# Attention steps of 512 score columns: nine steps a head pair in place of twelve, with the scan's state kept as a column

## The chip, the core and the metric

The kernel runs on one core of a Trainium2 chip. The metric is device time in microseconds (us) of one execution. The core has a matrix engine (TensorE, PE in the profile, with its weight loads as PEld), three engines for elementwise work (VectorE or DVE, ScalarE or ACT, GpSimd or POOL) and a queue that issues the transfers (SyncE or SP). PE writes to PSUM alone; POOL works on SBUF alone.

## The reference, cut to what matters

A trunk of two layers over 1024 positions of width 1024: a Mamba-2 layer, a shared projection to K and V, and one layer of stick-breaking attention with 16 heads of 64, then a norm. The change touches the attention alone. For each block of 128 queries:

```python
z = jnp.einsum('bthd,bshd->bhts', q[:, lo:hi], k[:, :hi]) * scale
mask = (query position > key position)
log_keep = jnp.where(mask, jax.nn.log_sigmoid(-z), 0.0)
after = lax.cumsum(log_keep, axis=3, reverse=True) - log_keep
log_a = jnp.where(mask, jax.nn.log_sigmoid(z) + after, -jnp.inf)
a = jnp.exp(log_a)
outs.append(jnp.einsum('bhts,bshd->bthd', a, v[:, :hi]))
```

The weight of a key is thus sigmoid(z) times the product of sigmoid(-z) over all later keys that the query may see. The kernel computes that product as a running product (a scan) from the last key to the first.

## The kernel before, in words

Everything ahead of the attention (about the first 1010 us) and behind it is the same in both kernels.

**Work of the attention.** Heads go in eight pairs p. A pair has eight query blocks i of 128 queries, and the keys are cut into two halves c of 512. A *piece* (i, c) is block i against half c: block 6 has the pieces (6,1), 384 columns wide, and (6,0), 512 wide; block 2 has (2,0) alone, 384 wide. The piece that holds the diagonal is a *top* piece; for a block with two pieces the upper half (c = 1) is done first, since the running product goes from the last key down. A pair has twelve pieces with 36 x 128 columns.

**A step** is one piece in `scores` (L819) and, LAG = 3 steps later, in `transposes` (L849).
- `scores`: PE multiplies for both heads into the PSUM tile `sc` (L828; one buffer of two banks). ACT reads it twice, sigmoid(-z) into `kp` (L830) and sigmoid(z) into `be` (L831). For a top piece POOL masks the diagonal 128 columns of both (L835) and sets the end column of `kp` to 1 (L837). For the other pieces it copies the first column of the upper piece's `kp` into that place (L839). DVE scans `kp` in place, once for each head (L841); the scan of a lower piece starts from the first column of the upper one's `kp`, which `above` remembers as a whole tile. POOL multiplies `be` with `kp` shifted by one column (L846).
- `transposes`: PE transposes the 128-column blocks of `be` into a PSUM tile `at` for each head (L856; two buffers). ACT empties the first head's (L860), DVE the second's (L858), into the SBUF tile `aT` of the block pair t = i // 2.
- `av` (L862): one step after the last piece of a block pair has been transposed, PE multiplies `aT` with V (L869), and DVE multiplies the result with the gate (L872).

**Filler.** Between these, PE runs the projections to queries and gates (`qproj` L768, `zproj1` L780), and at the end part of the output projection (`oproj` L794), as a generator: each `next` is one *yield* of three matmuls with 512 columns. For each weight, ACT makes the rounded copy and POOL the residual (`lq`, `lqz`, L124 and L125, four pieces each).

**Order.** PE's order is the program's (a manual schedule); the other engines' instructions are ordered by the compiler's scheduler. The main loop (L905) does for step n, with `rate` = `rates[n % 12]`:

```python
transposes(...)                      # of step n - 3
for _ in range((rate + 1) // 2): next(fl, None)
for r in now: av(*r[1])
live[n] = scores(p, i, c)
for _ in range(rate // 2): next(fl, None)
```

The `order` of pieces and `rates` (L900 to L902) are written out by hand and sum up to 32 yields a pair.

Of the kernel before, what the change touches and what calls it, by code (L numbers as in the profile page):

```python
# [12 lines left out]
F32 = mybir.dt.float32  # L13
F32R = mybir.dt.float32r
AF = mybir.ActivationFunctionType
ALU = mybir.AluOpType
# [3 lines left out]
P = 128  # L20
# [4 lines left out]
HT = T // NH  # L25
# [7 lines left out]
AVD = 1  # L33
# [19 lines left out]
def tile_trunk(ctx, tc, xT, c, vec, ada0, adar, wxbc, wwave, wdt, wz, wmo, wk, wv, wq, wqz, wso, out):  # L53
    nc = tc.nc
    V, S, Q, E, Y = nc.vector, nc.scalar, nc.gpsimd, nc.tensor, nc.sync
# [58 lines left out]
    def mm_tile(name):  # L114
        return pmm.tile([P, HT], F32, tag="mm", name=name)
# [43 lines left out]
    with ExitStack() as es:  # L159
# [9 lines left out]
                        channel_multiplier=-1)  # L169
# [97 lines left out]
        def wave_mm(d, hf):  # L267
            for m in range(NW):
# [12 lines left out]
                               op1=ALU.mult)  # L281
# [148 lines left out]
        order = []  # L430
# [23 lines left out]
    with ExitStack() as es:  # L454
# [30 lines left out]
        st = [pst.tile([P, 512], F32, name=f"st{g}") for g in range(G)]  # L485
# [128 lines left out]
        for n, (i, cc) in enumerate(todo):  # L614
            u = units[i]
            c = u["hf"] * CPH + cc
# [28 lines left out]
    with ExitStack() as es:  # L645
# [27 lines left out]
        for hf in range(NH):  # L673
# [3 lines left out]
            for d in range(ND):  # L677
# [19 lines left out]
            ps = pp.tile([P, HT], F32, tag="ss", name=f"ss1_{hf}")  # L697
# [15 lines left out]
        for hf in range(NH):  # L713
            hs = slice(hf * HT, (hf + 1) * HT)
            for m in range(8):
                wh, wl = load_w(wk[m], f"k{m}_{hf}")
                ps = mm_tile(f"pk{m}_{hf}")
# [7 lines left out]
            for ch in range(2):  # L725
                ps = [pp.tile([P, 512], F32, tag=f"v{s}", name=f"pv{s}_{ch}_{hf}") for s in range(4)]
# [35 lines left out]
    with ExitStack() as es:  # L762
        pa = pool(es, "p5", bufs=2)
        pp = pool(es, "pp5", bufs=2, space=PSUM)
        pone = pp.tile([P, 1], F32, name="pone", bufs=1)
# [50 lines left out]
        hsl = [slice(64 * a, 64 * a + 64) for a in range(2)]  # L816


        def scores(p, i, c):  # L819
            kd, q = pairs[p][0], qs[p]  # L820
            n = f"{p}_{i}_{c}"
            w = min(P * (i + 1), HT * (c + 1)) - HT * c
            top = HT * c + w == P * (i + 1)
# [3 lines left out]
            for a in range(2):  # L827
                E.matmul(ps[:, a, 0:w], q[hsl[a], i * P:(i + 1) * P], kd[hsl[a], HT * c:HT * c + w],  # L828
                         start=True, stop=True)
            S.activation(kp[:, :, 0:w], ps[:, :, 0:w], AF.Sigmoid, scale=-0.125)  # L830
            S.activation(be[:, :, 0:w], ps[:, :, 0:w], AF.Sigmoid, scale=0.125)  # L831
            if top:
                dg = slice(w - P, w)
                for t, fill in ((kp, 1.0), (be, 0.0)):
                    Q.affine_select(out=t[:, :, dg], in_=t[:, :, dg], pattern=[[0, 2], [-1, P]],  # L835
                                    compare_op=ALU.is_gt, fill=fill, base=0, channel_multiplier=1)
                Q.memset(kp[:, :, w:w + 1], 1.0)  # L837
            else:
                Q.tensor_copy(kp[:, :, w:w + 1], above[p, i][:, :, 0:1])  # L839
            for a in range(2):  # L840
                V.tensor_tensor_scan(out=kp[:, a, 0:w][:, ::-1], data0=kp[:, a, 0:w][:, ::-1],  # L841
                                     data1=pone.to_broadcast([P, w]),
                                     initial=1.0 if top else above[p, i][:, a, 0:1], op0=ALU.mult,
                                     op1=ALU.mult)
            above[p, i] = kp
            Q.tensor_tensor(out=be[:, :, 0:w], in0=be[:, :, 0:w], in1=kp[:, :, 1:w + 1], op=ALU.mult)  # L846
            return be

        def transposes(p, i, c, be, at):  # L849
            n = f"{p}_{i}_{c}"  # L850
            m = min(i + 1 - 4 * c, 4)
            tc_ = slice((i % 2) * P, (i % 2 + 1) * P)
            for a in range(2):
                ps = pp.tile([P, 4, P], F32, tag="at", name=f"at{n}_{a}", bufs=2)
                for j in range(m):
                    E.transpose(ps[:, j, :], be[:, a, j * P:(j + 1) * P], ident)  # L856
                if a:
                    V.tensor_copy(at[:, a, 0:m, tc_], ps[:, 0:m, :])  # L858
                else:
                    S.copy(at[:, a, 0:m, tc_], ps[:, 0:m, :])  # L860

        def av(p, t, at):  # L862
            vd, g = pairs[p][1], gs[p]
# [18 lines left out]
        qs, szs, pairs, gs, above = {}, {}, {}, {}, {}  # L882
# [20 lines left out]
        steps = [(p, *ic) for p in range(8) for ic in order]  # L903
        live, rows, ready = {}, {}, []
        for n in range(len(steps) + LAG + AVD):  # L905
            rate = rates[n % 12]
            m = n - LAG
            now, ready = [r for r in ready if r[0] <= n], [r for r in ready if r[0] > n]
            if 0 <= m < len(steps):
                p, i, c = steps[m]  # L910
                t = i // 2
                if (p, t) not in rows:
                    rows[p, t] = [pa.tile([P, 2, 4, 256], F32, tag="aT", name=f"aT{p}_{t}_{b}", bufs=3)
                                  for b in range((2 * t + 5) // 4)]
                transposes(p, i, c, live.pop(m), rows[p, t][c])
                if i % 2 == 1 and c == 0:
                    ready.append((n + AVD, (p, t, rows.pop((p, t)))))
            for _ in range((rate + 1) // 2):
                next(fl, None)
            for r in now:  # L920
                av(*r[1])
            if n < len(steps):
                p, i, c = steps[n]
                if n % 12 == 0:
# [3 lines left out]
                live[n] = scores(p, i, c)  # L928
            for _ in range(rate // 2):
                next(fl, None)  # L930
        for _ in fl:
# [3 lines left out]
    with ExitStack() as es:  # L935
# [25 lines left out]
        for hf, c0, c1, ds in ((1, 0, 512, (0, 5, 1, 2, 3, 4, 6, 7)), (0, 0, 256, (6, 7, 0, 1, 2, 3, 4, 5)),  # L961
                               (0, 256, 512, (6, 7, 0, 1, 2, 3, 4, 5))):
            w = c1 - c0
            last = hf == 0 and c0 > 0
            n = f"{hf}_{c0}"
# [6 lines left out]
            for i, d in enumerate(ds):  # L972
                if hf == 0:
                    t = x2t[:, i, :]
                elif d < NPRE:
                    t = x2p[d]
                else:
                    t = pf.tile(sh, F32, tag=f"x2_{d}", name=f"x2_{d}", bufs=1)
                if hf == 0 or d >= NPRE:
                    Y.dma_start(out=t, in_=x1_d[d][hf][:, c0:c1])  # L980
                if hf == 1 and d == NPRE:
                    ps = part[d][0]
                elif hf == 1 and d < NPRE:
                    ps = mm_tile(f"ps{d}_{n}")
                else:
                    ps = pp.tile([P, HT], F32, tag="pq", name=f"ps{d}_{n}", bufs=4)[:, 0:w]
# [4 lines left out]
                else:  # L991
# [3 lines left out]
                    for k in range(ND):  # L995
# [3 lines left out]
                                       op1=ALU.add)  # L999
# [93 lines left out]
```

## Time and profile before

| | us |
|---|---|
| median of three runs | 1516.09 (1509.9 to 1516.46) |
| the profiled execution's own time | 1520.12 |
| its span in the profile | 1518.4 |
| attention stage, first scores to last product | about 1012 to 1440 of the span |
| PE busy in the whole span | 1450.6 |

Engines are named as above. In the views, a group of instructions has the line of the kernel, the engine, the operation and its tiles (out<-in), and a row's bracket tells how long the engine had been idle before it and what ended that. Matmuls are pipelined, and the ends that the profile gives them are modelled, so a row's duration for a matmul is longer than the distance to the next matmul's start. An f32 matmul is recorded as two.

### The profile page before, as it was taken

The page shows a single profiled execution, that of the slowest core. Times are in us where ns is not written, and L with a number is a line of the kernel's source. Part 1 is how long each engine was busy: PE and PEld are TensorE (multiplying, and loading weights), DVE is VectorE, ACT ScalarE, POOL GpSimd, SP SyncE. Part 2 cuts the span into 40 slices and gives each one's busy share as a digit, 9 for nine tenths or more (in the row PEclk, how much of TensorE's full clock was granted, in tenths as well). Part 3 has the DMA queues.
Part 4 walks back from the last instruction along what each step waited for, and adds up shares of the span by engine and source line. Part 5 has one row for each costly group of instructions (what it writes and reads, how often), then busy time and mean ns, then how long its engine had stood idle before and what let it go on. Part 6 is the DMA issues. An engine that isn't in the chain of part 4 may idle for free.

```text
span 1518.4 us, 20697 instructions
## 1 busy us (share of the span) xinstructions
PE 1450.6 (96%) x7538; PEld 1113.8 (73%) x7538; DVE 989.7 (65%) x1221; ACT 746.4 (49%) x1273; POOL 563.1 (37%) x613
## 2 busy tenths in 40 slices
PE   4799999999998899999999999999999999999997
PEld 2587887888776788788888888876666666666787
DVE  5989974545789888976733427225665666667564
ACT  5554446235767666733523325244454545455542
POOL 2821220002655566522011000046565656556532
PEclk8899999999999999999999999999999999999999
DMA  9278884234566766658433446441121212112252
GB/s 337 86 247 292 286 297 153 98 110 127 180 219 211 215 213 211 197 170 285 151 121 124 139 139 193 130 141 43 49 77 43 62 44 70 36 37 89 82 186 101
DMA packets 104581, 227.36 MB, mean 150 GB/s; under 512 B 9488, under 2 KB 40992, under 8 KB 103456
## 3 DMA queue, kind: packets, MB, share of 16 engines
q1 hardware_dynamic: 104480, 226.04, 45.4%
q8 instruction: 60, 0.98, 0.3%
q14 instruction: 41, 0.34, 0.1%
HBM read 184.32 MB, written 41.68 MB: 149 GB/s over the span
## 4 chain that ended last, share of the span: by engine, by line
PE 60%; DVE 10%; issue 4%; POOL 4%; ACT 3%; DMA 2%; DVEq 0%; POOLq 0%; ACTq 0%; SPq 0%
DVE kp L841 4%; PE av L869 4%; PE po L132 4%; PE po L130 4%; PE po L131 4%; PE sc L828 3%; PE at L856 3%; PE pr L132 2%; PE pz L130 2%; PE pr L131 2%; PE pr L130 2%; PE pk L130 2%; PE pv L137 2%; PE pk L132 2%; PE pv L135 2%
## 5 line engine op out<-in xcount | busy, mean ns | idle before, releaser
L846 POOL TENSOR_TENSOR be<-be,kp 128x768 f32<-128x768 f32 (+3 forms) x96 | 148.6, 1548 | 149.2 <-DVE kp L841 128.4
L830 ACT ACTIVATE kp<-sc 128x768 f32<-128x768 f32 (+3 forms) x96 | 78.3, 815 | 183.7 <-PE sc L828 157.2
L841 DVE TENSOR_TENSOR_SCAN kp<-kp,pone 128x512 f32<-128x512 f32 (+3 forms) x128 | 97.9, 807 | 80.6 <-POOL kp L835 79.6
L130 PE MATMUL pr<-h0h,hx 128*128 128x512 f32 x336 | 131.8, 392 | 5.0 <-ACT hx L124 2.5
L132 PE MATMUL pr<-h0h,lx 128*128 128x512 f32 x336 | 131.7, 392 | 0.5 <-DVE lx L125 0.5
L131 PE MATMUL pr<-h0l,hx 128*128 128x512 f32 x336 | 131.5, 391 | 0.0
L505 ACT ACTIVATE lm<-lm,nac 128x128 f32<-128x128 f32 x256 | 78.6, 389 | 57.9 <-POOL lm L502 57.9
L130 PE MATMUL pz<-h0h,hz 128*128 128x512 f32 x256 | 105.9, 414 | 0.0
L841 DVE TENSOR_TENSOR_SCAN kp<-kp,kp,pone 128x512 f32<-128x512 f32 x64 | 78.5, 1268 | 40.4 <-ACT kp L830 40.4
L132 PE MATMUL po<-yh,lo 128*128 128x512 f32 x256 | 101.0, 395 | 1.3 <-DVE lo L125 1.3
L131 PE MATMUL po<-yl,ho 128*128 128x512 f32 x256 | 101.5, 397 | 0.5 <-DVE yl L665 0.5
L130 PE MATMUL po<-yh,ho 128*128 128x512 f32 x256 | 100.7, 393 | 1.3 <-ACT ho L124 1.3
L132 PE MATMUL pz<-h0h,lz 128*128 128x512 f32 x256 | 100.5, 392 | 1.0 <-DVE lz L125 1.0
L131 PE MATMUL pz<-h0l,hz 128*128 128x512 f32 x256 | 100.1, 391 | 0.0
L125 POOL TENSOR_TENSOR lq<-rq,hq 128x256 fp32r<-128x256 f32 x32 | 22.7, 739 | 178.4 <-ACT hq L124 178.4
L856 PE MATMUL at<-ident,be 128*128 128x128 f32 x576 | 82.5, 277 | 6.3 <-POOL be L846 5.0
L828 PE MATMUL sc<-kd,q 64*128 64x512 f32 (+3 forms) x384 | 88.0, 535 | 0.0
L533 POOL TENSOR_TENSOR xwl<-xw,xwh 128x512 fp32r<-128x512 f32 x20 | 26.8, 1341 | 163.2 <-ACT xwh L531 153.6
L856 PEld LDWEIGHTS at<-ident,be 128*128 128x128 f32 x576 | 66.1, 141 | 25.3 <-POOL be L846 8.0
L340 DVE SCALAR_TENSOR_TENSOR cv<-pr,vt,cv 128x1023 f32<-128x1023 f32 (+2 forms) x63 | 80.4, 1277 | 0.9
L124 ACT CAST ho<-ro 128x1024 fp32r<-128x1024 f32 x32 | 33.7, 1053 | 89.9 <-PE po L131 81.3
L130 PEld LDWEIGHTS pr<-h0h,hx 128*128 128x128 f32 x336 | 63.5, 189 | 19.1 <-ACT hx L124 2.9
(258 smaller groups left out, 3921.6 us busy)
## 6 DMA issues: line engine op xcount, KB each, us to landing
ar<-adar SPq DMA_DIRECT2D x48, 512.0 KB, 5.3
lm<-ac_d SPq DMA_DIRECT2D x32, 512.0 KB, 4.9
rz<-wz SPq DMA_DIRECT2D x32, 512.0 KB, 3.9
ro<-wmo SPq DMA_DIRECT2D x32, 512.0 KB, 3.5
xs_d<-sv SPq DMA_DIRECT2D x24, 512.0 KB, 3.4
rx<-wxbc SPq DMA_DIRECT2D x21, 512.0 KB, 4.9
x<-xT SPq DMA_DIRECT2D x32, 256.0 KB, 5.4
a<-ada SPq DMA_DIRECT2D x8, 1024.0 KB, 7.4
```

What stands on the lines that cost most here:

```text
L124: S.copy(h[:, i:i + n, :], r[:, i:i + n, :])
L130: E.matmul(ps, wh, xh, start=first, stop=False)
L131: E.matmul(ps, wh, xl, start=False, stop=False)
L132: E.matmul(ps, wl, xh, start=False, stop=last)
L340: V.scalar_tensor_tensor(out=ac[:, i:], in0=ps[:, :T - i], scalar=vv("cw", m * 4 + 3 - i), in1=ac[:, i:], op0=ALU.mult, op1=ALU.add)
L505: S.activation(lm[:, h, :], lm[:, h, :], AF.Exp, bias=nac[:, c, h0_ + h:h0_ + h + 1])
L828: E.matmul(ps[:, a, 0:w], q[hsl[a], i * P:(i + 1) * P], kd[hsl[a], HT * c:HT * c + w], start=True, stop=True)
L830: S.activation(kp[:, :, 0:w], ps[:, :, 0:w], AF.Sigmoid, scale=-0.125)
L841: V.tensor_tensor_scan(out=kp[:, a, 0:w][:, ::-1], data0=kp[:, a, 0:w][:, ::-1], data1=pone.to_broadcast([P, w]), initial=1.0 if top else ...
L846: Q.tensor_tensor(out=be[:, :, 0:w], in0=be[:, :, 0:w], in1=kp[:, :, 1:w + 1], op=ALU.mult)
L856: E.transpose(ps[:, j, :], be[:, a, j * P:(j + 1) * P], ident)
L869: E.matmul(ps[hsl[a], cs], vd[:, j, hsl[a]], at[j // 4][:, a, j % 4, cs], start=j == 0, stop=j == nj - 1)
```

## The change

Pieces are put together so that each step has exactly 512 columns: (6,1) with (0,0), (1,0) with (5,1), (4,1) with (2,0), and six pieces that are 512 wide alone. A generator `pieces` gives for each piece of a step its width w, its offset o in `sc` and `be`, its offset ok in `kp` (one column more for each piece, for its end column) and whether it is a top piece. In `scores`, PE, the first sigmoid, masks, scans and products go piece by piece; the second sigmoid covers the whole step. For an upper piece POOL copies the first column of its scan into a small tile of its own, which takes the place of the whole `kp` in `above`. In `transposes` four blocks are transposed for each head, and the evictions go piece by piece. The tiles `aT` have four buffers in place of three and are allocated one by one. The order and the rates are new. The diff, cut to its core:

```diff
+        def pieces(step):
+            o = 0
+            for b, (i, c) in enumerate(step):
+                w = min(P * (i + 1), HT * (c + 1)) - HT * c
+                yield i, c, w, o, o + b, HT * c + w == P * (i + 1)
+                o += w
+
-        def scores(p, i, c):
+        def scores(p, step):
...
-            kp = pa.tile([P, 2, HT + 1], F32, tag="kp", name="kp" + n, bufs=3)
+            kp = pa.tile([P, 2, HT + 2], F32, tag="kp", name="kp" + n, bufs=3)
...
-            S.activation(kp[:, :, 0:w], ps[:, :, 0:w], AF.Sigmoid, scale=-0.125)
-            S.activation(be[:, :, 0:w], ps[:, :, 0:w], AF.Sigmoid, scale=0.125)
...
+            for i, c, w, o, _, _ in pieces(step):
+                for a in range(2):
+                    E.matmul(ps[:, a, o:o + w], q[hsl[a], i * P:(i + 1) * P],
+                             kd[hsl[a], HT * c:HT * c + w], start=True, stop=True)
+            for _, _, w, o, ok, _ in pieces(step):
+                S.activation(kp[:, :, ok:ok + w], ps[:, :, o:o + w], AF.Sigmoid, scale=-0.125)
+            S.activation(be, ps, AF.Sigmoid, scale=0.125)
+            for i, c, w, o, ok, top in pieces(step):
+                end = kp[:, :, ok + w:ok + w + 1]
+                if top:
...
+                else:
+                    Q.tensor_copy(end, above[p, i])
+                for a in range(2):
+                    ka = kp[:, a, ok:ok + w][:, ::-1]
+                    V.tensor_tensor_scan(out=ka, data0=ka, data1=pone.to_broadcast([P, w]),
+                                         initial=1.0 if top else above[p, i][:, a, 0:1], op0=ALU.mult,
+                                         op1=ALU.mult)
+                if c == 1:
+                    above[p, i] = pa.tile([P, 2, 1], F32, tag="ab", name=f"ab{p}_{i}", bufs=5)
+                    Q.tensor_copy(above[p, i], kp[:, :, ok:ok + 1])
+                Q.tensor_tensor(out=be[:, :, o:o + w], in0=be[:, :, o:o + w],
+                                in1=kp[:, :, ok + 1:ok + w + 1], op=ALU.mult)
...
-                for j in range(m):
+                for j in range(4):
                     E.transpose(ps[:, j, :], be[:, a, j * P:(j + 1) * P], ident)
...
+                for i, c, w, o, _, _ in pieces(step):
...
+                    at = rows[p, t][c][:, a, 0:m, (i % 2) * P:(i % 2 + 1) * P]
+                    if a:
+                        V.tensor_copy(at, ps[:, o:o + m, :])
+                    else:
+                        S.copy(at, ps[:, o:o + m, :])
...
-        order = [(6, 1), (6, 0), (7, 1), (7, 0), (0, 0), (1, 0), (4, 1), (4, 0), (5, 1), (5, 0), (2, 0),
-                 (3, 0)]
-        rates = (3, 4, 4, 4, 1, 1, 1, 4, 2, 3, 2, 3)
...
+        order = [((6, 1), (0, 0)), ((6, 0),), ((7, 1),), ((7, 0),), ((1, 0), (5, 1)), ((4, 1), (2, 0)),
+                 ((4, 0),), ((5, 0),), ((3, 0),)]
+        rates = (4, 4, 4, 4, 2, 4, 4, 3, 3)
```

## Rows read from the trace of the kernel before

**Rows 1.** The page, first part: busy us of each engine, share, instructions

```profile
PE 1450.6 (96%) x7538; PEld 1113.8 (73%) x7538; DVE 989.7 (65%) x1221; ACT 746.4 (49%) x1273; POOL 563.1 (37%) x613
```

**Rows 2.** Windows: two periods of one head pair, and four us in the seventh

```profile
core 0: us, PE busy (x) PEld busy (x) DVE busy (x) ACT busy (x) POOL busy (x), PEclk, DMA share, GB/s
...
1109.45:1161.51 52.06, 51.37 (x298) 33.32 (x296) 31.79 (x45) 26.46 (x46) 30.78 (x49) 1.00 0.18 57
1161.51:1213.58 52.07, 51.38 (x298) 33.33 (x297) 31.80 (x45) 26.46 (x46) 30.79 (x49) 1.00 0.19 55
...
1372.00:1376.00 4.00, 3.34 (x14) 2.35 (x16) 4.00 (x4) 2.90 (x5) 3.08 (x3) 0.73 0.06 23
```

**Rows 3.** Timeline of PE around the step after piece (0,0): start us, us, what

```profile
1130.29 0.47 PE L130 MATMUL pq<-h1h,hq 128*128 128x512 f32 x1
...
1131.16 0.49 PE L828 MATMUL sc<-kd,q 64*128 64x128 f32 x4
1131.58 0.66 PE L856 MATMUL at<-ident,be 128*128 128x128 f32 x4
1132.40 0.66 PE L856 MATMUL at<-ident,be 128*128 128x128 f32 x4 [0.16 <-DVE aT L858]
1132.81 0.48 PE L130 MATMUL pq<-h1h,hq 128*128 128x512 f32 x1
```

**Rows 4.** Timeline of PE up to the transposes of piece (2,0) and behind

```profile
1157.53 0.50 PE L130 MATMUL pqz<-h1h,hqz 128*128 128x512 f32 x1
...
1158.33 1.04 PE L856 MATMUL at<-ident,be 128*128 128x128 f32 x8
1159.12 0.48 PE L130 MATMUL pqz<-h1h,hqz 128*128 128x512 f32 x1
...
1160.67 0.92 PE L828 MATMUL sc<-kd,q 64*128 64x384 f32 x4
1161.51 0.50 PE L130 MATMUL pqz<-h1h,hqz 128*128 128x512 f32 x1
...
1163.00 0.88 PE L856 MATMUL at<-ident,be 128*128 128x128 f32 x6 [0.53 <-POOL be L846]
...
1167.73 0.70 PE L828 MATMUL sc<-kd,q 64*128 64x512 f32 x2
```

**Rows 5.** Timeline of PE at the same place of the seventh pair

```profile
1369.78 0.50 PE L130 MATMUL pqz<-h1h,hqz 128*128 128x512 f32 x1
...
1372.66 0.88 PE L856 MATMUL at<-ident,be 128*128 128x128 f32 x6 [1.92 <-POOL be L846]
...
1378.96 1.13 PE L828 MATMUL sc<-kd,q 64*128 64x512 f32 x4
```

**Rows 6.** Timelines of DVE and POOL before piece (2,0)'s transposes; line 754: ns min/median/max

```profile
1159.45 1.80 DVE L841 TENSOR_TENSOR_SCAN kp<-kp,pone 128x384 f32<-128x384 f32 x2 [3.84 <-POOL kp L835]
...
1156.20 2.12 POOL L125 TENSOR_TENSOR lq<-rq,hq 128x256 fp32r<-128x256 f32 x3
...
L754 DVE TENSOR_TENSOR gl<-gr,gh x14: 667/684/2491, 1364.4 to 1453.7; 128x512 fp32r<-128x512 f32 x14
```

**Rows 7.** Groups by form in the period 1109.45 to 1161.51: busy us, mean ns

```profile
L831 ACT ACTIVATE be<-sc 128x1024 f32<-128x1024 f32 x6 | 6.1, 1019 | 0.0
...
L835 POOL TENSOR_SCALAR_AFFINE_SELECT kp<-kp 128x256 f32<-128x256 f32 x8 | 3.3, 413 | 0.3 <-ACT kp L830 0.3
...
L841 DVE TENSOR_TENSOR_SCAN kp<-kp,pone 128x256 f32<-128x256 f32 x4 | 2.5, 675 | 1.5 <-POOL kp L835 1.4
...
L846 POOL TENSOR_TENSOR be<-be,kp 128x512 f32<-128x512 f32 x2 | 2.2, 1090 | 2.2 <-DVE kp L841 2.2
...
L830 ACT ACTIVATE kp<-sc 128x512 f32<-128x512 f32 x2 | 1.2, 600 | 2.9 <-PE sc L828 2.9
...
L839 POOL COPY kp<-kp 128x2 f32<-128x2 f32 x4 | 0.8, 188 | 0.0
```

**Rows 8.** The chain of waits: the product with V of blocks 6 and 7

```profile
1138.28 3.39 PE av L869 x32
```

More of the change, by code (lines that the diff above doesn't have):

```diff
@@ L825, in scores @@
             be = pa.tile([P, 2, HT], F32, tag="be", name="be" + n, bufs=4)
             ps = pp.tile([P, 2, HT], F32, tag="sc", name="sc" + n, bufs=1)
-            for a in range(2):
-                E.matmul(ps[:, a, 0:w], q[hsl[a], i * P:(i + 1) * P], kd[hsl[a], HT * c:HT * c + w],
-                         start=True, stop=True)
-            S.activation(kp[:, :, 0:w], ps[:, :, 0:w], AF.Sigmoid, scale=-0.125)
-            S.activation(be[:, :, 0:w], ps[:, :, 0:w], AF.Sigmoid, scale=0.125)
[L832 to L846, printed above, removed]
-            return be
@@ new lines, in scores @@
+            S.activation(be, ps, AF.Sigmoid, scale=0.125)
+            for i, c, w, o, ok, top in pieces(step):
+                end = kp[:, :, ok + w:ok + w + 1]
+                if top:
+                    for t, e, fill in ((kp, ok + w, 1.0), (be, o + w, 0.0)):
+                        t = t[:, :, e - P:e]
+                        Q.affine_select(out=t, in_=t, pattern=[[0, 2], [-1, P]],
+                                        compare_op=ALU.is_gt, fill=fill, base=0, channel_multiplier=1)
+                    Q.memset(end, 1.0)
+                else:
[10 more added lines that the diff above has]
+                                in1=kp[:, :, ok + 1:ok + w + 1], op=ALU.mult)
@@ L853, in transposes @@
+            return be
+        def transposes(p, step, be):
+            n = f"{p}_{step[0][0]}_{step[0][1]}"
             for a in range(2):
                 ps = pp.tile([P, 4, P], F32, tag="at", name=f"at{n}_{a}", bufs=2)
-                for j in range(m):
+                for j in range(4):
                     E.transpose(ps[:, j, :], be[:, a, j * P:(j + 1) * P], ident)
[L857 to L860, printed above, removed]
+                for i, c, w, o, _, _ in pieces(step):
+                    t, m, o = i // 2, w // P, o // P
+                    if (p, t) not in rows:
+                        rows[p, t] = {}
+                    if c not in rows[p, t]:
+                        rows[p, t][c] = pa.tile([P, 2, 4, 256], F32, tag="aT", name=f"aT{p}_{t}_{c}",
+                                                bufs=4)
+                    at = rows[p, t][c][:, a, 0:m, (i % 2) * P:(i % 2 + 1) * P]
[3 more added lines that the diff above has]
+                        S.copy(at, ps[:, o:o + m, :])
@@ L899, in tile_trunk @@
             next(fl)
-        order = [(6, 1), (6, 0), (7, 1), (7, 0), (0, 0), (1, 0), (4, 1), (4, 0), (5, 1), (5, 0), (2, 0),
-                 (3, 0)]
-        rates = (3, 4, 4, 4, 1, 1, 1, 4, 2, 3, 2, 3)
-        steps = [(p, *ic) for p in range(8) for ic in order]
+        order = [((6, 1), (0, 0)), ((6, 0),), ((7, 1),), ((7, 0),), ((1, 0), (5, 1)), ((4, 1), (2, 0)),
+                 ((4, 0),), ((5, 0),), ((3, 0),)]
+        rates = (4, 4, 4, 4, 2, 4, 4, 3, 3)
+        ns = len(order)
+        steps = [(p, st) for p in range(8) for st in order]
         live, rows, ready = {}, {}, []
         for n in range(len(steps) + LAG + AVD):
-            rate = rates[n % 12]
+            rate = rates[n % ns]
             m = n - LAG
@@ L909, in tile_trunk @@
             if 0 <= m < len(steps):
[L910 to L917, printed above, removed]
+                p, st = steps[m]
+                transposes(p, st, live.pop(m))
+                for i, c in st:
+                    if i % 2 == 1 and c == 0:
+                        ready.append((n + AVD, (p, i // 2, rows.pop((p, i // 2)))))
             for _ in range((rate + 1) // 2):
@@ L922, in tile_trunk @@
             if n < len(steps):
-                p, i, c = steps[n]
-                if n % 12 == 0:
+                p, st = steps[n]
+                if n % ns == 0:
                     gs[p] = pa.tile([P, T], F32, tag="g", name=f"g{p}", bufs=1)
@@ L927, in tile_trunk @@
                         pairs[p + 1] = load_pair(p + 1)
-                live[n] = scores(p, i, c)
+                live[n] = scores(p, st)
             for _ in range(rate // 2):
```

8 lines of the change are left out of this document (1 added, 7 removed).

## The prediction

> **What bounds the kernel now.** I read the page first, then the attention stage pair by pair, then TensorE's own queue. The page has PE (TensorE) busy for 96% of the span [rows 1]. A busy PE is not proof of a full one, so the second view cuts the attention stage into head pairs. From the second pair on the pattern repeats every 52.06 us (six periods, all 52.04 to 52.09; two stand here): PE is busy for 51.4 us of it, DVE (VectorE) for 31.8, POOL (GpSimd) for 30.8, ACT (ScalarE) for 26.5 [rows 2]. Third, the PE timeline, read by start times and not by durations: what counts is the distance from the first matmul of a burst to the first of the next.
> - A filler burst of three projection matmuls (one yield) that runs up to a score burst takes 1131.16 - 1130.29 = 0.87 us [rows 3], one of six takes 1160.67 - 1159.12 = 1.55 [rows 4]. So a yield is 0.68 us and entering and leaving the burst costs 0.19.
> - Up to transposes, a burst of one yield takes 1158.33 - 1157.53 = 0.80 [rows 4].
> - The scores of one piece: 0.42 us for 128 columns [rows 3], 0.84 for 384 [rows 4], which is 0.21 for each 128 columns and 0.21 fixed per piece.
> - Eight transposes: 1159.12 - 1158.33 = 0.79 [rows 4].
>
> Two places of each period are longer than that. In the step after piece (0,0) the transposes take 1132.81 - 1131.58 = 1.23 us, 0.44 more than 0.79: PE stops in the middle until DVE has emptied one of the two transposed-score buffers [rows 3]. And the transposes of (2,0) start 1163.00 - 1161.51 = 1.49 us after the filler before them, 0.69 more than 0.80: POOL's product is late [rows 4]. Behind that stand POOL's queue, where the weight residuals of the next projection (lq) come first, and DVE's scan, which was idle for 3.84 us until POOL's mask [rows 6]. Everything else on PE starts as soon as the instruction before it allows. So PE sets the pace, with 1.13 us of waiting in 52.06.
>
> Once, in the seventh pair, the second wait is larger: 1372.66 - 1369.78 - 0.80 = 2.08 us, and behind it the granted clock is at 0.73 for 4 us (a mean of the two levels, 1.2 and 2.4 GHz) [rows 2, 5]. From those transposes to the next scores takes 1378.96 - 1372.66 = 6.30 us [rows 5] where the same work took 1167.73 - 1163.00 = 4.73 [rows 4]: 1.57 us lost to the clock. That place costs 3.65 us in all.
>
> **The change, part by part.**
>
> *Nine steps for twelve.* No matmul goes: twelve pieces a pair are still scored one by one (0.21 us fixed each), 72 blocks are transposed, and the 32 yields a pair are the same (both lists of rates add up to 32). What goes is three visits to the filler: a step asks for (rate+1)//2 yields before its scores and rate//2 behind them. Before, the three steps with rate 1 have only the first, so there are 12 + 9 = 21 bursts; after, 9 + 9 = 18. Three bursts at 0.19 us are 0.57 us a pair, 4.6 us in eight pairs, all on PE and so on the path.
>
> *Two pieces in one score burst.* No row shows this. From below, the second piece hides its fixed 0.21 us in the first: 3 x 8 x 0.21 = 5.0 us gained. From above, it pays it twice: 5.0 lost. Pieces pay 0.21 whether filler or transposes follow [rows 3, 4], so I take no difference, and keep both ends.
>
> *Transposes in fours.* The number is the same, and eight always fill the two buffers. Evictions stay one per piece and head, so ACT and DVE do what they did. But the steps that were short, (0,0), (1,0) and (4,1) with one yield each, are gone: the shortest step is now 3.72 us long ((1,0)+(5,1): 0.79 transposes, 0.87 filler, 1.26 scores, 0.80 filler), so DVE has that long to empty a buffer. I let the 0.44 us go: 8 x 0.44 = 3.5 us. If it stays, these 3.5 stay.
>
> *The late product of (2,0).* It had the time from its scores to its transposes three steps later. By the same burst lengths that stretch is 10.3 us at its shortest after the change ((7,0): 1.48 filler, then the steps of 3.72 and 5.08), and 10.75 for (1,0)+(5,1): 0.80 filler, then (4,1)+(2,0) at 0.79 + 1.55 + 1.26 + 1.48 = 5.08 and (4,0) at 4.87. Now (2,0) has 13.9 us: 1.48, 4.87, and a step of 7.58 into which the 3.39 us product of the probabilities of blocks 6 and 7 with V falls [rows 8]. So its wait goes: six pairs at 0.69 are 4.1 us. What is late next would be (1,0)+(5,1), with two diagonals on POOL. Its chain from below: first sigmoid 0.60, mask 0.41, four scans of 256 columns at 0.68, product 1.09: 4.8 us [rows 7]. From above, with nothing side by side: sigmoids 0.60 + 0.60 + 1.02, four masks 1.65, two end columns and the kept column at 0.19 each (at most a copy's time), scans 2.70, products 2.18, and four lq of 0.71 in front (2.12 for three), 2.83: 12.15 us, 1.4 over its 10.75, or 11.2 us in eight pairs [rows 6, 7]. Before, engines did work side by side here (the scan of (2,0) ran beside PE, ACT and POOL's next mask), so I take the lower half: no wait.
>
> *The large wait in the seventh pair.* By the same slack I let it go, with the clock behind it: 3.65 us. There DVE also splits the gates that come back from memory (L754), in 667 to 2491 ns for the same shape [rows 6]. The Trainium skill, SBUF — State Buffer, section Who interferes with whom, has DVE instructions with two SBUF inputs and POOL instructions that read SBUF exclude each other; the spread of that row agrees. By that rule the collision is still there after the change and the 3.65 stay, which would make the sum 12.2 and not 15.9.
>
> *The kept column.* Four copies a pair of 0.19 us more on POOL [rows 7]: 0.8 us on an engine that works 30.8 of 52.06. The copy waits for the scans of its piece, and behind it on POOL wait this piece's product, which needs the same scans, and the masks of a second piece. Who waits for it is the scan of the lower half of the same block, a step of 4.87 us later. Cost: nothing; without that cover 32 x 0.19 = 6.1 us.
>
> *Fewer second sigmoids.* ACT loses three instructions a pair and computes the same columns; it is idle for half of the time. Nothing. The fourth probability buffer and the wider scan tile add no instruction. No DMA moves, and SP's queue is not touched.
>
> **The sum**, against the profiled execution's own 1520.12 us (span 1518.4, 1.7 around it): 4.6 + 3.5 + 4.1 + 3.65 = 15.9 us, which gives 1504.2; a period of 52.06 - 0.57 - 0.44 - 0.69 = 50.36 us. The profiled execution stands 4.0 us above the median of the three runs (1516.09), so against the median 1500.2: **1500 us**.
>
> **Rivals.**
> 1. *The waits stay, or others of their size replace them.* Only the 4.6 us come: 1515.5 by the profiled execution, 1511.5 against the median. For it: the transposed-score buffers are still two and the masked ones four, and 12.15 us of chain against 10.75 would give back 11.2 us, about what the two repeating waits and the large one bring (3.5 + 4.1 + 3.65 = 11.25). Against it: the steps that were too short are gone. The Trainium skill, Perfetto Trace Analysis, section Optimization Strategy, reads a gap that repeats as a sign that a buffer for the next tile is missing; by that rule both repeating waits would stay. The row with DVE's eviction agrees for the 0.44, the one with POOL's product does not show a buffer.
> 2. *Slower: POOL is late at (1,0)+(5,1) in every pair.* Masks, two products and lq follow one another in one queue there. If PE then waits as long as it did in the seventh pair, with the clock behind it, each pair pays 3.65 us, 29.2 in all: 1529. It decides from 2.9 us a pair on (the 15.9 gained and the 7.6 of the threshold, over eight). Against it: the chain's upper bound is over by only 1.4.
> 3. *The steps were the pace.* If each step had a length of its own, nine would take 9/12 of 52.06, 39.0 us a pair: about 1412. PE's 51.4 busy us and its start times speak against it.
>
> **How the numbers follow.** Forecast 0.66, rival 1 0.19, rival 2 0.13, rival 3 0.02. The likeliest gives 1500. The range goes down to 1494 (the lowest run lies 6.2 under the median; the score bursts could give 5.0) and up to 1512 (rival 1's 1511.5, which is also above the forecast with a score burst 5.0 dearer). A measurement of this kernel tells about 0.5%, 7.6 us, from no change: faster is below 1508.5, which holds the forecast and rival 3 (0.68); rival 1 is the same (0.19); rival 2 slower (0.13).
>
> **What would show it.** In the windows a period of about 50.4 us with PE busy for nearly all of it. In the PE timeline no idle before transposes, the second piece's scores 0.42 to 0.63 us behind the first's, eighteen filler bursts a pair. In the groups 72 second sigmoids, all 128x1024, and 32 more column copies on POOL. Wrong would be a wait of PE for POOL's product at (1,0)+(5,1), PE waiting for DVE's evictions once a pair as before, or a granted clock under 1.00 in the stage more than once.

## The result and the profile after

The changed kernel takes 1498.9 us (median of four runs, 1495.8 to 1502.4) against 1515.75 (four runs): the ratio is 0.9891, 95% interval 0.9872 to 0.9911. The profiled execution took 1502.42 us, 17.7 less than that of before. From the first to the last score matmul the attention stage is 390.76 us long where it was 409.30; the 0.8 us that are missing between 18.5 and 17.7 lie outside it, where the code is the same. That outside part differs from execution to execution: in the profiled executions of this document the first scores start anywhere between 1003.7 and 1011.7 us. So the experiments are read by the period of one head pair, which repeats to a few hundredths of a us, and not by one execution's time.

The windows of the changed kernel, two periods and then the first half of the eighth pair's steps (the rows of before are [rows 2]):

```profile
core 0: us, PE busy (x) PEld busy (x) DVE busy (x) ACT busy (x) POOL busy (x), PEclk, DMA share, GB/s
...
1105.28:1155.05 49.77, 49.77 (x297) 33.86 (x297) 31.08 (x45) 25.98 (x43) 32.98 (x52) 1.00 0.19 59
1155.05:1204.82 49.77, 49.77 (x297) 33.87 (x296) 31.09 (x45) 25.98 (x43) 32.98 (x52) 1.00 0.20 58
...
1354.14:1379.50 25.36, 23.45 (x138) 15.72 (x137) 21.91 (x26) 14.96 (x25) 16.14 (x22) 1.00 0.25 79
```

The period is 49.77 us and PE is busy in all of it: nothing is waited for any more, in all six undisturbed pairs. The clock stays at 1.00 throughout. POOL does 33.0 us a pair where it did 30.8.

The PE timeline around the steps (1,0)+(5,1) and (4,1)+(2,0), to be read by start times (before: [rows 3, 4]):

```profile
1127.54 0.48 PE L130 MATMUL pq<-h1h,hq 128*128 128x512 f32 x1
...
1128.41 1.13 PE L835 MATMUL sc<-kd,q 64*128 64x256 f32 x8
1129.47 0.50 PE L130 MATMUL pq<-h1h,hq 128*128 128x512 f32 x1
...
1130.27 1.04 PE L867 MATMUL at<-ident,be 128*128 128x128 f32 x8
1131.07 0.47 PE L130 MATMUL pq<-h1h,hq 128*128 128x512 f32 x1
...
1132.63 1.14 PE L835 MATMUL sc<-kd,q 64*128 64x128 f32 x8
1133.70 0.50 PE L130 MATMUL pq<-h1h,hq 128*128 128x512 f32 x1
```

The transposes take 0.80 us and follow their filler at once. And the score bursts of two pieces take 1129.47 - 1128.41 = 1.06 and 1133.70 - 1132.63 = 1.07 us, where the prediction had 1.26. One piece of 512 columns alone takes 1.06 too. The fixed 0.21 us is paid by the burst, not by the piece.

PE's waits in the whole stage, in us, times, longest:

```profile
PE at L867 <- DVE aT L877: 1.1, 1, 1.1
PE sc L835 <- ACT be L839: 0.8, 1, 0.8
```

Both stand in the eighth pair. PE's timeline there (before: [rows 5]), ACT's just ahead, and the residuals of the reloaded gate blocks, ns min/median/max (before: [rows 6]):

```profile
1357.49 0.48 PE L130 MATMUL pqz<-h1h,hqz 128*128 128x512 f32 x1
...
1359.95 1.13 PE L835 MATMUL sc<-kd,q 64*128 64x512 f32 x4 [0.82 <-ACT be L839]
...
1362.51 0.60 PE L867 MATMUL at<-ident,be 128*128 128x128 f32 x4
1364.20 0.66 PE L867 MATMUL at<-ident,be 128*128 128x128 f32 x4 [1.09 <-DVE aT L877]
1364.62 0.48 PE L130 MATMUL pqz<-h1h,hqz 128*128 128x512 f32 x1
```

```profile
1356.62 1.39 ACT L753 CAST gh<-gr 128x512 fp32r<-128x512 f32 x2
1357.90 1.08 ACT L838 ACTIVATE kp<-sc 128x768 f32<-128x768 f32 x2
```

```profile
L754 DVE TENSOR_TENSOR gl<-gr,gh x14: 664/686/2674, 1350.3 to 1435.8; 128x512 fp32r<-128x512 f32 x14
```

The filler before the scores lasts 2.46 us and not 1.56, the transposes 1364.62 - 1362.51 = 2.11 and not 0.79. That is 0.90 + 1.32 = 2.2 us, in the stretch in which ACT makes the rounded copies of the gate blocks (two of them stand right before the sigmoids that free the score buffer) and DVE their residuals.

Two groups of the changed kernel by form, busy us and mean ns: the second sigmoid in the period from 1105.28, and POOL's product over the whole span (2004 ns before, over as many):

```profile
L839 ACT ACTIVATE be<-sc 128x1024 f32<-128x1024 f32 x9 | 9.2, 1023 | 0.0
...
L858 POOL TENSOR_TENSOR be<-be,kp 128x1024 f32<-128x1024 f32 x48 | 105.2, 2191 | 86.5 <-DVE kp L852 67.5 <-PE pq L132 10.4 <-DVE aT L877 6.7
```

The nine second sigmoids are as foreseen. The product is 9% slower, which nothing in the change explains at first sight.

### The profile page after: what moved, and what is told of

Read it like the earlier page. It is cut to its first block, busy times and chain, and to the rows that moved or that the text cites. A ratio compares the mean times of both kernels' runs of the same rounds, so it can differ in the third digit from the quotient of the medians.

```text
span 1500.7 us, 20592 instructions
## 1 busy us (share of the span) xinstructions
PE 1435.7 (96%) x7538; PEld 1115.1 (74%) x7538; DVE 991.1 (66%) x1221; ACT 742.3 (49%) x1249; POOL 582.6 (39%) x645
## 4 chain that ended last, share of the span: by engine, by line
PE 73%; DVE 5%; ACT 2%; DMA 2%; issue 1%; POOL 1%; DVEq 0%; SPq 0%; POOLq 0%; ACTq 0%
PE sc L835 5%; PE av L888 4%; PE at L867 4%; PE po L132 4%; PE po L130 4%; PE po L131 4%; PE pz L130 2%; PE pqz L130 2%; PE pq L130 2%; PE pz L132 2%; PE pz L131 2%; PE pr L132 2%; PE pq L132 2%; PE pr L130 2%; PE pr L131 2%; PE pq L131 2%
## 5 line engine op out<-in xcount | busy, mean ns | idle before, releaser
L858 POOL TENSOR_TENSOR be<-be,kp 128x1024 f32<-128x1024 f32 (+2 forms) x96 | 162.3, 1691 | 90.2 <-DVE kp L852 70.9
L838 ACT ACTIVATE kp<-sc 128x1024 f32<-128x1024 f32 (+2 forms) x96 | 75.5, 813 | 174.6 <-PE sc L835 172.0
L852 DVE TENSOR_TENSOR_SCAN kp<-kp,pone 128x128 f32<-128x128 f32 (+3 forms) x128 | 96.1, 803 | 69.2 <-POOL kp L845 69.2
L852 DVE TENSOR_TENSOR_SCAN kp<-kp,ab,pone 128x512 f32<-128x512 f32 x64 | 78.4, 1266 | 28.3 <-ACT kp L838 17.2
L835 PE MATMUL sc<-kd,q 64*128 64x512 f32 (+3 forms) x384 | 81.5, 522 | 0.8 <-ACT be L839 0.8
L353 POOL TENSOR_TENSOR ar<-ar,crow 128x1024 f32<-128x1024 f32 x12 | 30.9, 2572 | 119.5 <-DMA ar<-adar 119.5
L867 PE MATMUL at<-ident,be 128*128 128x128 f32 x576 | 74.7, 272 | 1.1 <-DVE aT L877 1.1
```

What stands on the lines that cost most here:

```text
L835: E.matmul(ps[:, a, o:o + w], q[hsl[a], i * P:(i + 1) * P], kd[hsl[a], HT * c:HT * c + w], start=True, stop=True)
L838: S.activation(kp[:, :, ok:ok + w], ps[:, :, o:o + w], AF.Sigmoid, scale=-0.125)
L852: V.tensor_tensor_scan(out=ka, data0=ka, data1=pone.to_broadcast([P, w]), initial=1.0 if top else above[p, i][:, a, 0:1], op0=ALU.mult, op ...
L858: Q.tensor_tensor(out=be[:, :, o:o + w], in0=be[:, :, o:o + w], in1=kp[:, :, ok + 1:ok + w + 1], op=ALU.mult)
```

## The experiments

The theory after the result: a period lost 2.29 us (52.06 to 49.77), made of 0.44 + 0.69 of waits, three score bursts at 0.21, and the 0.53 that is left, put down to three entries from the filler into scores. The residuals on DVE cost 2.2 us once. Each experiment changes one thing.

**The two pieces' scores apart.** One yield of filler is moved between them:

```diff
             for i, c, w, o, _, _ in pieces(step):
+                if o:
+                    for _ in range(gap):
+                        next(fl, None)
                 for a in range(2):
...
-                live[n] = scores(p, st)
-            for _ in range(rate // 2):
+                live[n] = scores(p, st, 1)
+            for _ in range(rate // 2 - (n < len(steps) and len(steps[n][1]) == 2)):
```

> The changed kernel, with one filler yield moved from behind the scores to between the scores of the two pieces of a step. Theory (the fixed 0.21 us is paid once per score burst, so a second piece in the same burst is free of it): three score bursts more and two filler bursts more a pair, 3 x 0.21 + 2 x 0.19 = 1.0 us, the period goes from 49.77 to 50.8 us and the profiled time from 1502.4 to about 1510.5. Rival (each piece pays 0.21 wherever it stands, and the extra gain came from elsewhere): only the two filler bursts, 0.38 us, period 50.15, about 1505.5.

The execution took 1507.6 us, the period is 50.92. Its windows and its PE timeline:

```profile
1091.61:1142.53 50.92, 50.92 (x298) 33.54 (x297) 31.11 (x45) 26.00 (x44) 33.15 (x52) 1.00 0.18 58
```

```profile
1127.74 0.70 PE L838 MATMUL sc<-kd,q 64*128 64x256 f32 x4
1128.37 0.50 PE L130 MATMUL pq<-h1h,hq 128*128 128x512 f32 x1
...
1129.27 0.70 PE L838 MATMUL sc<-kd,q 64*128 64x256 f32 x4
1129.90 1.09 PE L870 MATMUL at<-ident,be 128*128 128x128 f32 x8
```

Apart, the two pieces of 256 columns take 0.63 us each, 1.26 together; in one burst they took 1.06. The period grew by 1.15, near the theory's 1.0 and far from the rival's 0.38. So the merged score burst itself brings 0.2 us for each of three steps, 5 us in all. And 50.92 is what the kernel before would take without its two waits, 52.06 - 0.44 - 0.69 = 50.93: with twelve score bursts again, each entered from filler, nearly all that the merging saved on PE itself is gone, the 0.53 with it.

**The order alone.** The kernel before, with its twelve steps in the new order:

```diff
-        order = [(6, 1), (6, 0), (7, 1), (7, 0), (0, 0), (1, 0), (4, 1), (4, 0), (5, 1), (5, 0), (2, 0),
-                 (3, 0)]
-        rates = (3, 4, 4, 4, 1, 1, 1, 4, 2, 3, 2, 3)
+        order = [(6, 1), (0, 0), (6, 0), (7, 1), (7, 0), (1, 0), (5, 1), (4, 1), (2, 0), (4, 0), (5, 0),
+                 (3, 0)]
+        rates = (3, 1, 4, 4, 4, 1, 1, 2, 2, 4, 3, 3)
```

> The kernel before, twelve steps, with the pieces in the order of the changed kernel and rates (3,1,4,4,4,1,1,2,2,4,3,3), again 32 yields and 21 filler bursts. Theory (the merging brings the gain): filler bursts and score bursts are as before, the short steps are still there, and at least the 0.44 us wait for an eviction stays: period 51.4 us or more, up to above 52.06 if POOL's products come late with three steps of delay now shorter. Rival (the order alone takes the two waits away): period 50.9 us (52.06 - 1.13).

1519.1 us, a period of 52.09; windows, and PE's largest wait in the stage:

```profile
1082.91:1135.00 52.09, 50.97 (x297) 33.38 (x296) 31.69 (x46) 26.50 (x46) 30.91 (x48) 1.00 0.19 56
```

```profile
PE at L856 <- POOL kp L837: 6.7, 6, 1.1
```

```profile
1106.44 0.49 PE L828 MATMUL sc<-kd,q 64*128 64x128 f32 x4
1108.05 1.09 PE L856 MATMUL at<-ident,be 128*128 128x128 f32 x8 [1.12 <-POOL kp L837]
```

PE loses about as much a pair as before, but now in one place: the transposes behind the scores of (0,0) start 1108.05 - 1106.44 - 0.42 = 1.19 us late, for POOL, in each of six pairs. The wait for DVE's eviction, which I had expected to stay, does not show in these pairs. Before, it stood in these same transposes; that their lateness hides it here is argued and not shown. The new order moved the waits and took no time away. The gain needs the merging.

**No step with rate 1.** The kernel before, with two yields at least in each step:

```diff
-        rates = (3, 4, 4, 4, 1, 1, 1, 4, 2, 3, 2, 3)
+        rates = (3, 3, 3, 4, 2, 2, 2, 4, 2, 2, 2, 3)
```

> The kernel before, with rates (3,3,3,4,2,2,2,4,2,2,2,3), so that no step is without filler behind its scores. Theory (a filler burst costs about 0.13 to 0.19 us of its own; the 0.44 us wait comes from steps too short for DVE's evictions): three bursts more cost 0.4 to 0.57 us, the 0.44 goes, the wait for (2,0)'s product stays: period 52.0 to 52.2 us. Rival (filler bursts cost nothing, the waits were all): period 51.6 us (52.06 - 0.44) or less.

1516.05 us, a period of 51.93, a little under what was expected; windows and waits:

```profile
1084.31:1136.24 51.93, 51.44 (x298) 33.25 (x297) 31.32 (x45) 26.36 (x46) 30.66 (x49) 1.00 0.19 56
```

```profile
PE at L856 <- POOL be L846: 4.9, 7, 1.9
```

```profile
1369.00:1373.00 4.00, 3.55 (x25) 2.58 (x27) 4.00 (x4) 2.90 (x5) 3.09 (x4) 1.00 0.04 14
```

The wait for DVE's eviction is gone from the list and the one for POOL's product is as it was. So the 0.44 us came from steps too short for the evictions. Three more bursts behind scores cost 51.93 - (52.06 - 0.44) = 0.31 us, 0.10 each: less than I expected, and less than the 0.19 that the prediction put on a burst. What a burst costs depends on what stands on either side of it, which the next runs show. The longest wait, 1.92 us in the pair with the residuals, is the same as in the kernel before, but the clock stays at 1.00 behind it (the last window).

**All filler ahead of the scores.** Nine bursts a pair in place of eighteen, in the changed kernel:

```diff
-            for _ in range((rate + 1) // 2):
+            for _ in range(rate):
                 next(fl, None)
...
-            for _ in range(rate // 2):
-                next(fl, None)
```

> The changed kernel, with all yields of a step ahead of its scores and none behind: nine filler bursts a pair in place of eighteen. Theory (each burst that ends at transposes costs 0.80 - 0.68 = 0.12 us of its own, and PE is the bound): 9 x 0.12 = 1.1 us a pair, period 48.7 us, 8.6 us less in all, about 1490 by the median. Rival (scores then wait for ACT's reading of the one score buffer, or transposes, now right behind the scores, for POOL's product, since the time from scores to transposes is 1.5 us shorter): PE waits take it back, period 49.8 us or more.

1492.9 us, 0.9856 of the kernel before (0.9824 to 0.9887); the period is 49.22. Windows and PE timeline:

```profile
1088.63:1137.85 49.22, 49.22 (x297) 33.87 (x297) 31.83 (x45) 25.88 (x44) 32.94 (x53) 1.00 0.19 60
```

```profile
1114.02 1.13 PE L835 MATMUL sc<-kd,q 64*128 64x512 f32 x4
1115.08 1.09 PE L867 MATMUL at<-ident,be 128*128 128x128 f32 x8
1115.93 0.48 PE L130 MATMUL pq<-h1h,hq 128*128 128x512 f32 x1
```

In the six undisturbed pairs no wait came back. But it brought 0.55 us a pair, half of what I expected: transposes right behind scores take 0.85 us, 0.06 more than behind filler, nine times a pair. By that, the transposes behind (0,0) in the kernel before waited 1.23 - 0.85 = 0.38 us and not 0.44, and the three bursts of the run before this one cost 51.93 - (52.06 - 0.38) = 0.25 us, 0.08 each, nearer to this run's 0.06.

Outside those pairs the rival shows: PE waits once for POOL's product in the first pair, and in the eighth once for POOL's mask and, for 0.7 us, once for ACT:

```profile
PE at L867 <- POOL be L858: 1.6, 1, 1.6
PE at L867 <- POOL be L845: 0.9, 1, 0.9
```

**All filler behind the scores**, and the residuals on POOL (the edit of the next run):

```diff
-            for _ in range((rate + 1) // 2):
-                next(fl, None)
             for r in now:
...
-            for _ in range(rate // 2):
+            for _ in range(rate):
                 next(fl, None)
```

> The changed kernel, with all yields of a step behind its scores and none ahead, and the seven residuals on POOL. Theory (a filler burst that ends at scores or at the product with V costs 0.19 us, one that ends at transposes 0.12; nothing waits): nine of the first kind go, 1.7 us a pair, period 48.1 us, and the eighth pair's 2.2 us go too, about 15.5 us less than the changed kernel, 1483 by the median. Rival (scores wait for ACT's two readings of the one score buffer, above all behind (1,0)+(5,1) with its two yields, or the transition from transposes to scores costs what the burst did): period 49.2 us or more.

1498.45 us, 0.9893 of the kernel before (0.9867 to 0.9920); the period is 49.71. Windows and PE timeline:

```profile
1089.57:1139.28 49.71, 49.71 (x297) 34.79 (x296) 31.45 (x44) 26.40 (x45) 33.05 (x52) 1.00 0.19 59
```

```profile
1118.43 1.03 PE L868 MATMUL at<-ident,be 128*128 128x128 f32 x8
1119.39 1.73 PE L889 MATMUL av<-aT,vd 128*64 128x256 f32 x16
```

Again no wait in the undisturbed pairs (one of 0.6 us for ACT in the eighth); and no gain: the period is 49.71 where I expected 48.1, and the stage is 388.70 us long, where the residuals on POOL alone give 388.53 (next run). The rival's second form held, that the way from transposes to scores costs what the burst did. Eight transposes take 1119.39 - 1118.43 = 0.96 us when the product with V (or scores, the same) comes next, 0.17 more than before filler. Entering scores or the product costs 0.17 to 0.19 us, whatever stands in front. A filler burst ahead of scores is therefore free; a step is not.

**The residuals on POOL**, in the changed kernel:

```diff
-        V.tensor_tensor(out=lo, in0=g, in1=f(hi), op=ALU.subtract)
+        eng = Q if hf == 1 and k < 7 else V
+        eng.tensor_tensor(out=lo, in0=g, in1=f(hi), op=ALU.subtract)
```

> The changed kernel, with the residuals of the seven reloaded gate blocks (L754, those of the second half of the positions) computed on POOL and not on DVE. Theory (PE's two waits in the eighth pair, 0.90 + 1.32 = 2.2 us, come from these subtractions standing in DVE's queue and colliding with POOL's reads): the two waits go, 2.2 us less, and nothing else changes. Rival (POOL is then late with products there): PE waits for POOL in the same stretch for as long or longer.

1492.4 us in one execution; its stage is 388.53 us long from first to last scores, 2.23 less than 390.76. The window of the eighth pair:

```profile
1333.71:1383.49 49.78, 49.78 (x298) 33.87 (x297) 30.24 (x44) 31.73 (x58) 43.54 (x63) 1.00 0.25 80
```

The pair with the residuals now takes 49.78 us like all others, though POOL works 43.5 us of it. Both waits are gone, so the 2.2 us hung on where the residuals run. For DVE's eviction that is its own queue. For ACT the way is not shown: in this run ACT's order changed too, and one rounded copy, not two, stands right before the sigmoids of (4,1)+(2,0).

The same edit in the kernel before:

> The kernel before, with the residuals of the seven reloaded gate blocks (L754) on POOL and not on DVE. Theory (the large wait of the seventh pair comes from these subtractions on DVE, the clock's loss from the wait): 2.08 us become the 0.69 of the other pairs, the 1.57 behind it go, that pair's period goes from 55.0 back to 52.07 us. Rival (POOL, on which the product waits, is later still): 55 us or more.

The window from the product with V of one pair to that of the next, in the kernel before and in this run, and this run's wait:

```profile
1346.48:1401.51 55.03, 52.95 (x297) 34.05 (x296) 39.38 (x52) 30.57 (x56) 33.37 (x49) 0.97 0.20 63
1342.22:1398.29 56.07, 52.93 (x298) 34.39 (x297) 32.39 (x45) 30.91 (x56) 39.24 (x56) 0.97 0.19 61
```

```profile
PE at L857 <- POOL be L847: 3.0, 1, 3.0
```

The pair takes 56.1 us, more than the 55.0 it took before, PE's wait for the product is 3.0 us where it was 1.9, and the clock falls as it did (0.97 over both windows): the rival was right. The execution took 1518.5 us. Before the change POOL stood between the scores and the transposes with no time to spare, so what it was given there was waited for. After it, the same work found room.

**The kept column undone.** The scan starts from the upper piece's whole tile again:

```diff
-                    above[p, i] = pa.tile([P, 2, 1], F32, tag="ab", name=f"ab{p}_{i}", bufs=5)
-                    Q.tensor_copy(above[p, i], kp[:, :, ok:ok + 1])
+                    above[p, i] = kp[:, :, ok:ok + 1]
...
-            kp = pa.tile([P, 2, HT + 2], F32, tag="kp", name="kp" + n, bufs=3)
+            kp = pa.tile([P, 2, HT + 2], F32, tag="kp", name="kp" + n, bufs=4)
```

> The changed kernel without the kept column: the scan of the lower piece starts from the first column of the upper piece's whole tile, as before; the scan tile gets four buffers so that it lives long enough. Theory (the column costs PE nothing): 32 copies of 0.19 us leave POOL, 0.75 us a pair of its 33.0, the period stays 49.77 us to 0.1. Rival (the copy on POOL between scan and scan holds things up): period shorter by 0.2 us or more.

1495.7 us in one execution; windows:

```profile
1085.84:1135.63 49.79, 49.79 (x297) 33.86 (x297) 31.07 (x45) 26.02 (x44) 32.50 (x48) 1.00 0.19 59
```

The period is the same to 0.02 us. The column costs nothing and brings no time; what it saves is the fourth buffer that this run gives the scan tile.

**POOL's slower product.** The kernel before with 514 columns for each head's row in the scan tile, the changed kernel with 515, and the kernel before with the larger tile but rows of 513. The first two change the number in the tile's shape alone; the third:

```diff
-            kp = pa.tile([P, 2, HT + 1], F32, tag="kp", name="kp" + n, bufs=3)
+            kp = pa.tile([P, 2 * HT + 4], F32, tag="kp", name="kp" + n, bufs=3)
+            kp = kp[:, 0:2 * HT + 2].rearrange("p (a w) -> p a w", a=2)
```

> The kernel before, with the scan tile 514 columns wide per head and not 513, nothing else; all engines' instructions stand in the same order. Theory (the width of a head's row in the scan tile slows POOL's product): the 128x1024 product goes from 2.00 to about 2.19 us, the other forms by 9% too, and PE's wait for (2,0)'s product grows from 0.69 by some 0.1 to 0.3 us: period 52.1 to 52.4. Rival (something else in the changed kernel slows it): 2.00 us as before.

> The changed kernel, with the scan tile 515 columns wide per head and not 514, nothing else. Theory (as for the 514 columns in the kernel before): the product of 128x1024 goes back from 2.19 to 2.00 us and the period stays 49.77, since PE does not wait for it. Rival: 2.19 as it is.

> The kernel before, with a scan tile as large as one of 514 columns per head, of which the first 2 x 513 are used: a head's row keeps its 513 columns, all later addresses move as with 514. Theory (POOL's product depends on the distance of the two heads' rows): 2.00 us for 128x1024 as before, period 52.07. Rival (it depends on the addresses of the tiles): 2.19 us and a period of about 52.35.

The product's row in each of the three, in this order, one period of the first, and the two products of the step (1,0)+(5,1) in the second, from its POOL timeline:

```profile
L846 POOL TENSOR_TENSOR be<-be,kp 128x1024 f32<-128x1024 f32 x48 | 105.6, 2199 | 92.9 <-DVE kp L841 74.3 <-ACT hq L124 14.2 <-ACT hso L124 2.4
```

```profile
L858 POOL TENSOR_TENSOR be<-be,kp 128x1024 f32<-128x1024 f32 x48 | 105.2, 2192 | 88.5 <-DVE kp L852 67.9 <-PE pq L132 12.0 <-DVE aT L877 6.7
```

```profile
L847 POOL TENSOR_TENSOR be<-be,kp 128x1024 f32<-128x1024 f32 x48 | 96.3, 2007 | 73.4 <-DVE kp L842 53.0 <-ACT hq L124 14.4 <-ACT hso L124 2.4
```

```profile
1079.77:1132.13 52.36, 51.34 (x298) 33.30 (x297) 31.87 (x44) 26.42 (x46) 32.53 (x49) 1.00 0.18 56
```

```profile
1127.17 1.20 POOL L858 TENSOR_TENSOR be<-be,kp 128x512 f32<-128x512 f32 x1 [0.37 <-DVE kp L852]
...
1128.97 1.10 POOL L858 TENSOR_TENSOR be<-be,kp 128x512 f32<-128x512 f32 x1
```

With 514 the kernel before has the slow product too, and its period grows by 0.29 us, since there POOL is waited for. With 515 the changed kernel keeps it, which I had not expected. With rows of 513 in the larger tile the product is fast. So it depends on the distance of the two heads' rows, not on addresses behind the tile. But not on the distance alone: with 515 the second product of a merged step, which reads its row from column 258 on, takes 1.10 us, and the first, from column 1 on, 1.20; with 514 both take the longer time. Why stays open, and other distances were not tried. (That third run's period was 51.78 us, 0.3 under the kernel before; the scheduler put POOL's instructions in another order there, and this was not followed up.) The three executions took 1515.3, 1496.6 and 1521.1 us.

**Filler ahead and residuals on POOL together**, in the changed kernel:

> The changed kernel, with all yields of a step ahead of its scores and none behind (as in the run with one burst a step) and the seven residuals on POOL. Theory (both effects add up: 0.55 us a pair from the missing bursts, and the waits of one pair, 1.7 us, go): period 49.22 us in all pairs, about 6.1 us less than the changed kernel, ratio to the kernel before 0.985. Rival (POOL, on which the transposes now wait sooner, is late in the pair with the residuals): the pair with the residuals takes 51 us or more, no gain over the run with one burst alone.

1493.7 us, 0.9866 of the kernel before (0.9846 to 0.9886). An undisturbed period, and the pair with the residuals:

```profile
1137.95:1187.17 49.22, 49.22 (x298) 33.88 (x297) 31.83 (x45) 25.88 (x44) 32.94 (x53) 1.00 0.18 60
1334.83:1385.71 50.88, 49.37 (x297) 33.87 (x296) 30.10 (x42) 31.40 (x57) 42.98 (x62) 1.00 0.24 78
```

The rival was right that there is no gain over the run with filler ahead alone (its 51 us were not quite reached). The same window of that run, residuals on DVE:

```profile
1334.73:1385.63 50.90, 49.33 (x297) 33.88 (x297) 38.79 (x48) 31.47 (x57) 36.63 (x54) 1.00 0.25 76
```

The stages are 387.05 and 387.07 us long. In that pair PE waits 0.8 us for POOL's product and 0.7 for ACT; with the residuals on DVE it was 0.9 for POOL's mask and 0.7 for ACT. With filler ahead, transposes stand right behind the scores and have less slack. The two gains do not add. Of the versions measured four times, the one with all filler ahead of the scores has the lowest median, 0.9856 of the kernel before; the interval of this last one overlaps with it, so the two cannot be told apart, and the one execution with the residuals alone on POOL (1492.4) is not apart from them either.

## Why the prediction was right, point by point

The forecast (1500 against 1498.9 measured, a period of 50.36 against 49.77) came from PE's start times, and that reading held: PE was the bound, its waits were what could go, and the terms could be summed.

- *Nine steps for twelve, 0.57 us a pair*: the size held (0.53 is left for it when the other terms are taken from the 2.29, and the run with the scores apart, at 50.92, gave that back too), but the name was wrong. The prediction put 0.19 us on "entering and leaving the burst" of filler. Removing bursts ahead of scores brought nothing, and a burst behind scores costs 0.06 to 0.10. What costs 0.17 to 0.19 us is entering scores or the product with V, and a step enters scores once.
- *Two pieces in one score burst, no difference*: this term was mis-sized. The lower end of its bounds was the truth: 0.20 us a step, 24 steps, 4.8 us. The rows that the estimate rested on [rows 3, 4] each held one burst with one piece, so they could not tell a price per burst from a price per piece; the bounds, not the value, were what they supported.
- *Transposes in fours, 3.5 us*: right. The wait for DVE went, and the run without rate 1 showed that short steps had caused it; that run had three buffers for `aT`, so the fourth is not what did it. Of the 0.44, 0.06 was no wait: the 0.79 it was measured against stands behind filler, and these transposes stood behind scores.
- *The late product of (2,0), 4.1 us*: right. The run with the order alone shows that the slack came from merging: with twelve steps the wait only moved. (1,0)+(5,1), named as next, did not become late, although POOL's products were 9% slower than the rows said.
- *The large wait, 3.65 us*: mis-sized. It lost the clock's share (1.00 throughout) but 2.2 us stayed, so 1.4 came. "By the same slack I let it go" was the step that failed: the slack was POOL's, and what was late after the change were DVE's evictions, behind the residuals of the gate blocks, and ACT's sigmoids, behind their copies. Against an undisturbed period the pair with the residuals took 55.03 - 52.06 = 2.97 us more before, 1.57 of it the clock's, and 2.22 after: the waits themselves did not shrink. And that the clock held is one execution's finding: with the same wait it held in the run without rate 1 (1.92 us) and in the run with the larger tile (1.83 us) too, so the change is not shown to have won those 1.57. The Trainium skill, SBUF — State Buffer, section Who interferes with whom, has DVE instructions with two SBUF inputs and POOL instructions that read SBUF exclude each other, so that the residuals still collide after the change. The trace agrees: 664 to 2674 ns for one shape on DVE, and 1277 to 1297 for the same on POOL.
- *The kept column, nothing*: right, 0.02 us by the run without it.
- *Rival 1*, that the repeating waits stay: neither did. The Trainium skill, Perfetto Trace Analysis, section Optimization Strategy, says that a repeating gap can mean a missing buffer. This trace does not show one: both gaps went while the transposed-score buffers stayed two and the masked ones four. It was time that was missing, and a step of four blocks has it.

The terms as measured, in the profiled executions: 24 x (0.53 / 3 + 0.20) = 9.0, 3.5, 4.1, and 1.4, together 18.1, against 18.5 us of the stage. The 0.53 is itself a remainder of the period, so this sum tests little beyond the pair with the residuals.

That 1500 lies within 1.1 us of the median is in part luck. The score bursts gave 4.8 us that the sum did not have, the large wait 2.2 less than it had, and the part outside the stage, where nothing was changed, took 0.8 us of the gain back in the profiled executions. The mechanism was right in the main; the agreement of the total is closer than the terms earned.

## What to carry to other kernels

Where one engine sets the pace and its stream switches between kinds of work, read the distance between starts at each switch, on both sides: it tells what a step costs apart from its work, and that is what merging small steps saved here. Before giving an idle-looking engine more work, look at whether it stands between the two ends of a waited-for chain: the same edit on POOL took 2.2 us off one kernel, put 1.0 on another, and changed nothing in a third. And an estimate for an operation that no row shows is as good as its bounds; here the bound was the answer.

## What the runs showed of the hardware that I had not expected

- A score burst in f32 costs 0.21 us beyond its columns once, whether it holds one piece or two with weights of their own (1.06 us for one piece of 512 columns, 1.06 and 1.07 for two).
- POOL's product of two SBUF operands of 128x1024 takes 2.00 us when the two heads' rows of one operand are 513 columns apart, and 2.19 to 2.20 when they are 514 or 515 apart. With 515 the product of a second piece, from column 258 on, keeps the short time (1.10 us for 128x512, against 1.20 from column 1 on).
- How long eight transposes hold PE, start to start, depends on what comes next and before: 0.79 us between filler, 0.85 behind scores, 0.96 ahead of the product with V or scores.
